# Two weight slabs per modulation product instead of one, in a two-layer diffusion transformer kernel

## The chip, the cores and the metric

The kernel runs on one core of one Trainium2 chip. The metric is the device time of one launch in microseconds (us). Three runs of the kernel before gave 2456.32, 2459.8 and 2463.0 us; the median is 2459.8 us. In the tables TensorE is PE (its weight loads PEld), VectorE is DVE, ScalarE is ACT, GpSimd is POOL, and SyncE is SP, which issues the transfers (DMAs).

## What is computed

Two layers run over 512 latent tokens and 256 context tokens, with a model width of 1024. Each layer first makes six modulation vectors for the latent tokens and six for the context tokens (shift, scale and gate of two sub-layers) out of one conditioning vector each:

```python
silu_c = jax.nn.silu(c)
silu_cc = jax.nn.silu(c_ctx)
...
mx = (silu_c @ w_ada[i] + b_ada[i])[:, None, :]
mc = silu_cc @ w_ada[i] + b_ada[i]
sx1, ax1, gx1, sx2, ax2, gx2 = jnp.split(mx, 6, axis=-1)
...
hx = modulate(rmsnorm(x, norm1_g[i]), sx1, ax1)
...
x = x + gx1 * y_x
x = x + gx2 * sqrelu_mlp(modulate(rmsnorm(x, norm2_g[i]), sx2, ax2), w_mlp1[i], w_mlp2[i])
```

`w_ada[i]` is 1024 x 6144 float32. It is 24 slabs of 1024 x 256, of 1 MB each, for a layer, so 48 in all. Between them stand the large products: the input projection, a differential attention, a depthwise convolution, two gate projections, two output projections, and an MLP of width 4096.

## The kernel before

**Weights.** Every large weight is read in slabs of 1 MB. `load_slab` (line 84) issues the transfer into a buffer with the tag "raw" (named `r_...`), and then splits it in two halves: ACT copies a half to a rounded part (`h_...`), and DVE or POOL subtracts that from the raw half (`l_...`). Products take three passes (`mm3`, lines 104 to 106): L104 and L105 need only `h_...`, L106 needs `l_...`. The tags of `h_...` and `l_...` have two buffers each. A modulation slab is not split: `raw_slab` (line 79) loads it, into the same tag "raw", as `ada...`, and the products read it from there.

**The raw buffers.** From the gate projections of layer 0 to the end of its MLP the tag "raw" has two buffers (`state["nraw"]` is 2, set at line 857), shared by the weight slabs and the modulation slabs. A buffer that held a weight slab is free when its split is done (DVE or POOL reads it last). A buffer that held a modulation slab is free when its eight products on PE are done.

**One modulation slab** (`ada_slab`, line 209): load it; eight products of 32 columns by 256 into a PSUM bank, `adaps`; ACT copies that to SBUF, `adasb`; two transposes on PE into the other half of the bank; DVE sums four strips with two reductions and adds the bias.

**Where the slabs stand.** Slabs 0 to 7 of layer 0 come first of all. Slabs 8 to 15 stand in the middle of the eight gate slabs (`wg`, line 941), 16 to 19 at the four slabs of the attention's output projection (`wao`), and 20 to 23 at the convolution's two (`wco`). The 24 slabs of layer 1 stand in the MLP of layer 0: two after the first two slabs of `w_mlp1`, and then one after each slab of `w_mlp1` (product `f`) and `w_mlp2` (product `r`), until none is left. In layer 1 there are none.

**What sets the order.** The framework's scheduler, which simulates a timeline (line 1287), orders the instructions of each engine and hands out the buffers; each engine and the queue of SP then run in the order written. An MLP slab has 96 matrix instructions: 2 blocks of columns by 8 rows by 3 passes for 512 tokens, and as many for 256.

Of the kernel before, what the change touches and what calls it, by code (L numbers as in the profile page):

```python
# [14 lines left out]
P = 128  # L15
# [36 lines left out]
def trunk_kernel(  # L52
# [153 lines left out]
        L["A2"] = lpool.tile([P, 2, KT], F32, tag="A2", name=f"A2{i}")  # L206
        return L

    def ada_slab(i, L, s):

        mi = state["mi"]
        r = raw_slab(rows(w_ada[i], 256 * s, 256), f"ada{i}_{s}")
        ps = mi(f"adaps{i}_{s}")
        for k in range(KT):
            j = k % 4
            nc.tensor.matmul(ps[32 * j : 32 * j + 32, :256], cvec[:, k, :], r[:, k, :],
                             start=k < 4, stop=k >= 4, tile_position=(0, 32 * j))
        if state["nt"] == 3:
            sb = state["tp"].tile([P, 512], F32, tag="t2k", bufs=3, name=f"adasb{i}_{s}")[:, :256]
        else:  # L220
            sb = spool.tile([P, 512], F32, tag="dg", name=f"adasb{i}_{s}", bufs=1)[:, :256]
        nc.scalar.activation(out=sb, in_=ps[:, :256], func=AF.Copy)
        pc = ps[:, 256:512]
        for m in range(2):
            nc.tensor.transpose(pc[:, m * P : m * P + P], sb[:, m * P : m * P + P], ident)
        ad = L["ad"][:, :, 2 * s : 2 * s + 2]
        for q in range(2):
            nc.vector.tensor_reduce(
                out=ad[:, q], in_=pc.rearrange("p (m j r) -> p m j r", m=2, j=4)[:, :, :, q],
                axis=AX.X, op=ALU.add)  # L230
        nc.vector.tensor_tensor(
            out=ad, in0=ad,
            in1=L["cols"][:, R_BADA + 2 * s : R_BADA + 2 * s + 2].unsqueeze(1)
            .to_broadcast([P, 2, 2]),
            op=ALU.add)

    def ada_gain(L, which, ks=slice(0, KT)):
        par, r0, nm = ((1, R_N1, "A1"), (4, R_N2, "A2"))[which]
# [121 lines left out]
                (w_qk[0][:, k, :], w_qk[1][:, k, :]), k == 0, k == KT - 1)  # L360

    for q in range(4):
        ada_slab(0, L, 4 + q)
        ada_slab(0, L, q)
        ada_gain(L, 0, slice(2 * q, 2 * q + 2))
        for k in (2 * q, 2 * q + 1):
            for s, g in ((0, LAT), (1, CTXS)):
                nc.vector.tensor_scalar(XN[:, k, g], XN[:, k, g], L["A1"][:, s, k : k + 1],
                                        L["ad"][:, s, k : k + 1], ALU.mult, ALU.add)
                split(hh[:, k, g], hl[:, k, g], XN[:, k, g])  # L370
        if q:
            qk_part(2 * q - 2)
            qk_part(2 * q - 1)
# [13 lines left out]
    for i in range(DEPTH):  # L387
# [532 lines left out]
        for half, lst in ((1, ga), (0, gc)):  # L920
            for s in range(4):
                if (half, s) not in wg:
                    gate_slab(half, s)
                if half == 0 and s == 3:
                    for hg in branch[:4]:
                        branch_load(*hg)
                w = wg.pop((half, s))
                for m in range(2):
                    mb = 2 * s + m
                    t = g3(f"g{i}_{half}_{mb}")  # L930
                    lst[mb] = t
                    for g in groups:
                        W = g.stop - g.start
                        ps = ps_for(g, f"gt{i}_{half}_{mb}_{g.start}")
                        fm_block(ps[:, :W], w, m * P, lambda k: (hh[:, k], hl[:, k]), g)
                        bcol = R_BG + half * KT + mb
                        nc.scalar.activation(out=t[:, g], in_=ps[:, :W], func=AF.Sigmoid,
                                             bias=cols[:, bcol : bcol + 1])
                    some_taps(per_gate)
                    if m == 0 and not state.get("ada_done"):  # L940
                        ada_slab(i, L, 8 + 4 * half + s)


        cgr = [(0, SEQ, 0)] + ([] if last else [(SEQ + PAD, CTX, SEQ)])
# [55 lines left out]
            split(ah[:, h : h + r.shape[1], g], al[:, h : h + r.shape[1], g], r)  # L1000
        for s in range(4):
            w = load_slab(rows(w_attn_out[i], 256 * s, 256), f"wao{i}_{s}")
            if not state.get("ada_done"):
                ada_slab(i, L, 16 + s)
            for g in groups:
                W = g.stop - g.start
                for m in range(2):
                    mb = 2 * s + m
                    ps = ps_for(g, f"ya{i}_{mb}_{g.start}")
                    fm_block(ps[:, :W], w, m * P, lambda k: (ah[:, k], al[:, k]), g)  # L1010
                    nc.vector.tensor_tensor(out=ga[mb][:, g], in0=ga[mb][:, g], in1=ps[:, :W],
                                            op=ALU.mult)
# [15 lines left out]
        for s in range(2):  # L1028
            w = load_slab(w_conv_out[i][:, 512 * s : 512 * s + 512]
                          .rearrange("(k p) n -> p k n", p=P), f"wco{i}_{s}", shape=(CT, 512))  # L1030
            if not state.get("ada_done"):
                ada_slab(i, L, 20 + 2 * s)
                ada_slab(i, L, 21 + 2 * s)
# [98 lines left out]
        for cch in range(4):  # L1132
# [15 lines left out]
            for s0 in ((0, 2), (2, 3), (3, 4)) if cch == 0 else ((n, n + 1) for n in range(4)):  # L1148
                for s in range(*s0):
                    if (cch, s) not in w1:  # L1150
                        mlp1_slab(cch, s)
                ws = {s: w1.pop((cch, s)) for s in range(*s0)}
                for g in halves if cch == 0 and s0[0] == 0 else groups:
                    for s in range(*s0):
                        for m in range(2):
                            hidden(ws[s], 2 * s + m, m, g)
                if not last and ada_todo:
                    for _ in range(*s0):
                        ada_slab(i + 1, Ln, ada_todo.pop(0))
            fin = cch == 3  # L1160
            if fin and not last:
                ada_gain(Ln, 0)
# [16 lines left out]
                            (w[0][:, k, :], w[1][:, k, :]), k == 0, k == KT - 1)  # L1179

            def after(s):
                if not last and ada_todo:
                    ada_slab(i + 1, Ln, ada_todo.pop(0))
                if fin and not last:
                    nc.sync.dma_start(xs_d[i + 1][:, 2 * s : 2 * s + 2, :],
                                      X[:, 2 * s : 2 * s + 2, :])
                if fin and last:
                    for t in range(4):
                        ps = state["mi"](f"oT{s}_{t}")
                        for m in range(2):  # L1190
# [17 lines left out]
                 lambda: first.update(v=v_slab(i + 1, 0, nc.gpsimd))) if fin and not last else ())  # L1208
        if not last:
            while ada_todo:  # L1210
                ada_slab(i + 1, Ln, ada_todo.pop(0))
            state["ada_done"] = True
            ada_gain(Ln, 1)
            L = Ln
# [77 lines left out]
```

## Time and profile before

One execution was profiled. "Span" is the time from its first instruction to its last.

| | us |
|---|---|
| median of three runs | 2459.8 |
| profiled execution, device time | 2461.13 |
| its span | 2459.3 |
| mean granted clock of TensorE over the span | 0.978 of full |
| PE idle, longest waits by line: gate product for `l_wg` from POOL, 2 times | 26.9 |
| PE idle before the first `yc` product of layer 1, once | 6.4 |

In the timeline a row gives the start, the duration, the engine, the source line, the operation, what it writes and reads, its shape and how many were merged; in brackets stands how long the engine sat idle before it, and who released it. One product of 32 columns by 256 shows as two records. A row of the windows view gives, for a stretch of the span, the busy time of each engine with its number of instructions, the granted clock of TensorE (PEclk, 1.00 is full) and the share of the DMA engines.

### The profile page before, as it was taken

The numbers are of one execution on the slowest core, as the hardware profiler recorded it, in microseconds if no ns is written. First come the engines' busy times: TensorE is split into PE (matmuls) and PEld (weight loads), VectorE is DVE, ScalarE is ACT, GpSimd is POOL, SyncE is SP. The second block draws the span as 40 slices with busy tenths as digits, with TensorE's granted clock in tenths as the row PEclk, the third lists the DMA queues.
The fourth block names the chain that finished last, engine by engine and source line by source line (L and its number), as shares of the span: only waits on it lengthen the run. The fifth ranks groups of instructions, "written<-read, shape, count | busy, mean of one in ns | idle before, by whom it ended". The sixth has DMA issues, their size and how long they took to land. (4 is left out here: it accounts for less than half of the span.)

```text
span 2459.3 us, 36996 instructions
## 1 busy us (share of the span) xinstructions
PE 2332.2 (95%) x15034; PEld 2066.7 (84%) x15034; DVE 1341.4 (55%) x2307; ACT 946.8 (38%) x1839; POOL 745.3 (30%) x1038
## 2 busy tenths in 40 slices
PE   7999999979999999999999998999896989999999
PEld 6889988868878988888888997989875869888887
DVE  6767776589657452222222356676747966533333
ACT  5556565512324242231312345555641323522331
POOL 2856665150000042120211255666614000200100
PEclk9999999989999999999999999999998999999999
DMA  9101111124444233333333221111113323323322
GB/s 299 55 27 46 42 43 43 43 95 156 132 141 157 84 104 103 121 119 113 112 120 103 73 66 54 42 42 42 59 56 101 118 91 104 103 86 103 96 92 69
DMA packets 222186, 224.79 MB, mean 91 GB/s; under 512 B 5872, under 2 KB 212160, under 8 KB 221888
## 3 DMA queue, kind: packets, MB, share of 16 engines
q1 hardware_dynamic: 222016, 222.43, 28.5%
q8 instruction: 118, 1.93, 0.3%
q14 instruction: 52, 0.43, 0.1%
HBM read 208.73 MB, written 13.67 MB: 90 GB/s over the span
## 5 line engine op out<-in xcount | busy, mean ns | idle before, releaser
L104 PE MATMUL f<-h2h,h_w 128*128 128x512 f32 (+1 forms) x832 | 284.8, 345 | 1.3 <-ACT h2h L76 1.0
L104 PE MATMUL r<-fh,h_w 128*128 128x512 f32 (+1 forms) x832 | 285.5, 344 | 0.5 <-DVE X L1072 0.5
L105 PE MATMUL f<-h2l,h_w 128*128 128x512 f32 (+1 forms) x832 | 284.9, 343 | 0.9 <-POOL h2l L77 0.8
L105 PE MATMUL r<-fl,h_w 128*128 128x512 f32 (+1 forms) x832 | 283.2, 341 | 0.0
L106 PE MATMUL r<-fh,l_w 128*128 128x512 f32 (+1 forms) x832 | 283.2, 341 | 0.0
L106 PE MATMUL f<-h2h,l_w 128*128 128x512 f32 (+1 forms) x832 | 283.1, 342 | 0.0
L76 ACT ACTIVATE h_w<-r_w 128x1024 fp32r<-128x1024 f32 x128 | 128.7, 1052 | 314.0 <-PE r L105 131.1
L1141 POOL TENSOR_TENSOR fr<-fr 128x512 f32<-128x512 f32 (+1 forms) x104 | 93.1, 897 | 509.5 <-ACT fh L1140 509.5
L887 DVE SCALAR_TENSOR_TENSOR cacc<-z,cols,cacc 128x783 f32<-128x783 f32 (+1 forms) x240 | 203.4, 902 | 0.5
L104 PE MATMUL qk<-h_wqk,h1h 128*128 128x256 f32 x640 | 185.5, 292 | 8.7 <-ACT rw L479 4.2
L105 PE MATMUL qk<-l_wqk,h1h 128*128 128x256 f32 x640 | 182.6, 287 | 0.0
L104 PEld LDWEIGHTS f<-h2h,h_w 128*128 128x128 f32 x832 | 158.0, 191 | 25.1 <-ACT fh L1140 2.5
L1072 DVE SCALAR_TENSOR_TENSOR X<-r,ad,X 128x512 f32<-128x512 f32 (+1 forms) x104 | 64.9, 627 | 208.6 <-PE r L106 208.4
L106 PE MATMUL qk<-h_wqk,h1l 128*128 128x256 f32 x640 | 178.6, 287 | 0.0
L104 PEld LDWEIGHTS r<-fh,h_w 128*128 128x128 f32 x832 | 157.6, 190 | 23.9 <-issue 3.7
L105 PEld LDWEIGHTS f<-h2l,h_w 128*128 128x128 f32 x832 | 159.0, 191 | 20.0 <-POOL h2l L77 2.1
L658 ACT ACTIVATE e<-S,st,rqk 128x768 f32<-128x768 f32 (+1 forms) x160 | 144.9, 908 | 76.5 <-POOL st L655 73.6
L106 PEld LDWEIGHTS f<-h2h,l_w 128*128 128x128 f32 x832 | 158.8, 191 | 17.6
L106 PEld LDWEIGHTS r<-fh,l_w 128*128 128x128 f32 x832 | 157.7, 190 | 17.7
L105 PEld LDWEIGHTS r<-fl,h_w 128*128 128x128 f32 x832 | 157.9, 190 | 17.0
L77 DVE TENSOR_TENSOR l_w<-r_w,h_w 128x1024 fp32r<-128x1024 f32 x106 | 126.2, 1223 | 82.2 <-ACT h_w L76 80.5
L653 DVE TENSOR_REDUCE st<-S 128x1 f32<-128x768 f32 (+1 forms) x160 | 134.0, 846 | 60.3 <-PE S L651 59.1
(248 smaller groups left out, 6254.6 us busy)
## 6 DMA issues: line engine op xcount, KB each, us to landing
r_w<-in_w_mlp_dram SPq DMA_DIRECT2D x64, 1024.0 KB, 5.5
ada<-in_w_ada_dram SPq DMA_DIRECT2D x48, 1024.0 KB, 5.3
r_wqk<-in_w_in_dram SPq DMA_DIRECT2D x32, 512.0 KB, 5.4
r_wg<-in_w_in_dram SPq DMA_DIRECT2D x16, 1024.0 KB, 5.5
r_wv<-in_w_in_dram SPq DMA_DIRECT2D x8, 1024.0 KB, 5.5
r_wao<-in_w_attn_out_dram SPq DMA_DIRECT2D x8, 1024.0 KB, 5.1
r_wo<-in_w_out_dram SPq DMA_DIRECT2D x8, 1024.0 KB, 8.2
at_d<-uo SPq DMA_DIRECT2D x40, 128.0 KB, 1.7
```

The source lines that it names most:

```text
L76: nc.scalar.activation(out=hi, in_=src, func=AF.Copy)
L77: (lo_eng or nc.vector).tensor_tensor(out=lo, in0=src, in1=f32(hi), op=ALU.subtract)
L104: nc.tensor.matmul(ps, sh, mh, start=first, stop=False)
L105: nc.tensor.matmul(ps, sh, ml, start=False, stop=False)
L106: nc.tensor.matmul(ps, sl, mh, start=False, stop=last)
L653: nc.vector.tensor_reduce(out=st[:, m : m + 1], in_=S[:, :nkey], axis=AX.X, op=ALU.max, negate=True)
L658: nc.scalar.activation(out=e[:, :nkey], in_=S[:, :nkey], func=AF.Exp, scale=R[:, t, m : m + 1], bias=st[:, m : m + 1], accum_out=st[:, 2 + ...
L887: nc.vector.scalar_tensor_tensor(out=ca[cc][:, :CV], in0=zt[cc][:, t : t + CV], scalar=wcol, in1=ca[cc][:, :CV], op0=ALU.mult, op1=ALU.add)
L1072: nc.vector.scalar_tensor_tensor(out=X[:, mb, g], in0=ps[:, :W], scalar=gate[:, s, mb : mb + 1], in1=X[:, mb, g], op0=ALU.mult, op1=ALU.add)
L1141: nc.gpsimd.tensor_tensor(out=r[:, :W], in0=r[:, :W], in1=r[:, :W], op=ALU.mult)
```

## The change

Two slabs of `w_ada` are loaded and multiplied together. Their products go side by side into one bank (512 columns), one ACT copy of 512 columns follows, four transposes go to a second bank, and the sums are made for both slabs (in one set of two reductions and one addition where the slabs are neighbours, in two sets in the first stage, which pairs slab 4+q with slab q). The number of products, of transposes and of bytes stays. There are half as many copies.

Each call site now calls for two slabs at every second place: in the gate stage at the odd slabs, in the attention's output projection at the odd slabs, and in the MLP after the even slabs.

```diff
-    def ada_slab(i, L, s):
+    def ada_pair(i, L, ss):
...
-        r = raw_slab(rows(w_ada[i], 256 * s, 256), f"ada{i}_{s}")
-        ps = mi(f"adaps{i}_{s}")
-        for k in range(KT):
-            j = k % 4
-            nc.tensor.matmul(ps[32 * j : 32 * j + 32, :256], cvec[:, k, :], r[:, k, :],
-                             start=k < 4, stop=k >= 4, tile_position=(0, 32 * j))
+        rs_ = [raw_slab(rows(w_ada[i], 256 * s, 256), f"ada{i}_{s}") for s in ss]
+        nm = f"{i}_{ss[0]}"
+        ps = mi(f"adaps{nm}")
+        for n, r in enumerate(rs_):
+            for k in range(KT):
+                j = k % 4
+                nc.tensor.matmul(ps[32 * j : 32 * j + 32, 256 * n : 256 * n + 256], cvec[:, k, :],
+                                 r[:, k, :], start=k < 4, stop=k >= 4,
+                                 tile_position=(0, 32 * j))
...
-        nc.scalar.activation(out=sb, in_=ps[:, :256], func=AF.Copy)
-        pc = ps[:, 256:512]
-        for m in range(2):
+        nc.scalar.activation(out=sb, in_=ps, func=AF.Copy)
+        pc = mi(f"adaT{nm}")
+        for m in range(4):
             nc.tensor.transpose(pc[:, m * P : m * P + P], sb[:, m * P : m * P + P], ident)
...
+        runs = [(0, 4, ss[0])] if ss[1] == ss[0] + 1 else [(0, 2, ss[0]), (2, 4, ss[1])]
...
     for q in range(4):
-        ada_slab(0, L, 4 + q)
-        ada_slab(0, L, q)
+        ada_pair(0, L, (4 + q, q))
...
-                    if m == 0 and not state.get("ada_done"):
-                        ada_slab(i, L, 8 + 4 * half + s)
+                    if m == 0 and s % 2 and not state.get("ada_done"):
+                        ada_pair(i, L, (7 + 4 * half + s, 8 + 4 * half + s))
...
-            if not state.get("ada_done"):
-                ada_slab(i, L, 16 + s)
+            if s % 2 and not state.get("ada_done"):
+                ada_pair(i, L, (15 + s, 16 + s))
...
                 if not last and ada_todo:
-                    for _ in range(*s0):
-                        ada_slab(i + 1, Ln, ada_todo.pop(0))
+                    if s0[0] % 2 == 0:
+                        ada_pair(i + 1, Ln, (ada_todo.pop(0), ada_todo.pop(0)))
...
             def after(s):
-                if not last and ada_todo:
-                    ada_slab(i + 1, Ln, ada_todo.pop(0))
+                if not last and ada_todo and s % 2 == 0:
+                    ada_pair(i + 1, Ln, (ada_todo.pop(0), ada_todo.pop(0)))
```

**The queue of SP in the MLP.** Before, weight slabs and modulation slabs took turns; here from the last slab of the first `w_mlp1` chunk (`r_w1_0_0_3`) on. The brackets name the engine or the transfer whose semaphore the queue waits for.

```order
L90 DMA r_w1_0_0_3_10090<-in_w_mlp1_dram 128x8x256 [waits DMAHW7_49,DMAHW1_49,DVE_49]
L81 DMA ada1_3_10218<-in_w_ada_dram 128x8x256 [waits DMAHW1_49,DVE_49]
L90 DMA r_w2_0_0_0_10236<-in_w_mlp2_dram 128x8x256 [waits DMAHW0_49,PE_49]
L81 DMA ada1_4_10348<-in_w_ada_dram 128x8x256 [waits DMAHW3_49,DVE_49,Pool_49]
L90 DMA r_w2_0_0_1_10366<-in_w_mlp2_dram 128x8x256 [waits DMAHW2_49,PE_49]
L81 DMA ada1_5_10478<-in_w_ada_dram 128x8x256 [waits DMAHW5_49,DVE_49,Pool_49]
```

The same place with the change:

```order
L90 DMA r_w1_0_0_3_10050<-in_w_mlp1_dram 128x8x256 [waits DMAHW0_49,PE_49]
L90 DMA r_w2_0_0_0_10178<-in_w_mlp2_dram 128x8x256 [waits DMAHW1_49,PE_49]
L81 DMA ada1_4_10290<-in_w_ada_dram 128x8x256 [waits DMAHW2_49,DVE_49]
L81 DMA ada1_5_10292<-in_w_ada_dram 128x8x256 [waits DMAHW3_49,DVE_49,Pool_49]
L90 DMA r_w2_0_0_1_10321<-in_w_mlp2_dram 128x8x256 [waits DMAHW4_49,PE_49]
L90 DMA r_w2_0_0_2_10433<-in_w_mlp2_dram 128x8x256 [waits DMAHW5_49,PE_49]
```

Two weight slabs now follow two modulation slabs. The PE event that `r_w2_0_0_1` waits for is, before, the last product of `ada1_3`, which PE runs ahead of all of `r_w2_0_0_0`'s products; with the change it is the last product of `ada1_4`, which PE runs behind them. `r_w2_0_0_2` waits for the last product of `ada1_5`.

**PE at the same place.** Rows of one form and one output are merged (`x8`); `h_w2_0_0_0` is the weight slab just finished, `h_w2_0_0_1` the next one. Before, and the two transposes 22 instructions later:

```order
L106 MATMUL r0_0_1_512_10322<-fh0_0_7_9546,l_w2_0_0_0_10239 128x256
L216 MATMUL adaps1_4_10350<-ada1_4_10348,cvec_328 32x256 x8
L104 MATMUL r0_0_2_0_10374<-fh0_0_0_9532,h_w2_0_0_1_10368 128x512
L105 MATMUL r0_0_2_0_10374<-fl0_0_0_9533,h_w2_0_0_1_10368 128x512
L106 MATMUL r0_0_2_0_10374<-fh0_0_0_9532,l_w2_0_0_1_10369 128x512
```

With the change:

```order
L106 MATMUL r0_0_1_512_10264<-fh0_0_7_9498,l_w2_0_0_0_10181 128x256
L218 MATMUL adaps1_4_10294<-ada1_4_10290,cvec_328 32x256 x8
L218 MATMUL adaps1_4_10294<-ada1_5_10292,cvec_328 32x256 x8
L228 MATMUL adaT1_4_10313<-cst_75,adasb1_4_10311 128x128 x4
L104 MATMUL r0_0_2_0_10329<-fh0_0_0_9484,h_w2_0_0_1_10323 128x512
L105 MATMUL r0_0_2_0_10329<-fl0_0_0_9485,h_w2_0_0_1_10323 128x512
L104 MATMUL r0_0_3_0_10355<-fh0_0_0_9484,h_w2_0_0_1_10323 128x512
L105 MATMUL r0_0_3_0_10355<-fl0_0_0_9485,h_w2_0_0_1_10323 128x512
L104 MATMUL r0_0_2_512_10381<-fh0_0_0_9484,h_w2_0_0_1_10323 128x256
L105 MATMUL r0_0_2_512_10381<-fl0_0_0_9485,h_w2_0_0_1_10323 128x256
L104 MATMUL r0_0_3_512_10407<-fh0_0_0_9484,h_w2_0_0_1_10323 128x256
L105 MATMUL r0_0_3_512_10407<-fl0_0_0_9485,h_w2_0_0_1_10323 128x256
```

Both slabs' products and all four transposes now stand together between two weight slabs, and the passes that need only `h_...` (L104, L105) of four blocks come ahead of the first L106. The same picture stands at eleven places of layer 0's MLP, for the pairs (2,3) to (22,23).

**PE in the gate stage.** `gt` is the gate product, and `wg0_1_3` the gate slab under way; with the change:

```order
L106 MATMUL gt0_1_6_512_6744<-h1h_0_334,l_wg0_1_3_6712 128x256
L218 MATMUL adaps0_14_6781<-ada0_14_6777,cvec_328 32x256 x8
L218 MATMUL adaps0_14_6781<-ada0_15_6779,cvec_328 32x256 x8
L104 MATMUL gt0_1_7_0_6809<-h1h_0_334,h_wg0_1_3_6711 128x512
L105 MATMUL gt0_1_7_0_6809<-h1l_0_335,h_wg0_1_3_6711 128x512
```

Here the pair stands in the middle of a weight slab: 48 products of `wg0_1_3` (24 for 512 tokens, 24 for 256) are still behind it. The next slab, `r_wg0_0_0`, waits for the last product of `ada0_14`; before, it waited for a split on DVE.

More of the change, by code (lines that the diff above doesn't have):

```diff
@@ L218, in ada_slab @@
         if state["nt"] == 3:
-            sb = state["tp"].tile([P, 512], F32, tag="t2k", bufs=3, name=f"adasb{i}_{s}")[:, :256]
+            sb = state["tp"].tile([P, 512], F32, tag="t2k", bufs=3, name=f"adasb{nm}")
         else:
-            sb = spool.tile([P, 512], F32, tag="dg", name=f"adasb{i}_{s}", bufs=1)[:, :256]
-        nc.scalar.activation(out=sb, in_=ps[:, :256], func=AF.Copy)
-        pc = ps[:, 256:512]
-        for m in range(2):
+            sb = spool.tile([P, 512], F32, tag="dg", name=f"adasb{nm}", bufs=1)
@@ L225, in ada_slab @@
+        nc.scalar.activation(out=sb, in_=ps, func=AF.Copy)
+        pc = mi(f"adaT{nm}")
+        for m in range(4):
             nc.tensor.transpose(pc[:, m * P : m * P + P], sb[:, m * P : m * P + P], ident)
[L226 to L235, printed above, removed]
+        pcv = pc.rearrange("p (m j r) -> p m j r", m=4, j=4)
@@ new lines, in ada_pair @@
+        runs = [(0, 4, ss[0])] if ss[1] == ss[0] + 1 else [(0, 2, ss[0]), (2, 4, ss[1])]
+        for a, b, s in runs:
+            ad = L["ad"][:, :, 2 * s : 2 * s + b - a]
+            for q in range(2):
+                nc.vector.tensor_reduce(out=ad[:, q], in_=pcv[:, a:b, :, q], axis=AX.X, op=ALU.add)
+            nc.vector.tensor_tensor(
+                out=ad, in0=ad,
+                in1=L["cols"][:, R_BADA + 2 * s : R_BADA + 2 * s + b - a].unsqueeze(1)
+                .to_broadcast([P, 2, b - a]),
+                op=ALU.add)
@@ L1031, in trunk_kernel @@
             if not state.get("ada_done"):
-                ada_slab(i, L, 20 + 2 * s)
-                ada_slab(i, L, 21 + 2 * s)
+                ada_pair(i, L, (20 + 2 * s, 21 + 2 * s))
             for m in range(4):
@@ L1210, in trunk_kernel @@
             while ada_todo:
-                ada_slab(i + 1, Ln, ada_todo.pop(0))
+                ada_pair(i + 1, Ln, (ada_todo.pop(0), ada_todo.pop(0)))
             state["ada_done"] = True
```

## The prediction

> **What bounds the kernel now.** I read the page first: its table of busy time, and the slices of the span.
>
> ```profile
> PE 2332.2 (95%) x15034; PEld 2066.7 (84%) x15034; DVE 1341.4 (55%) x2307; ACT 946.8 (38%) x1839; POOL 745.3 (30%) x1038
> ...
> PEclk9999999989999999999999999999998999999999
> DMA  9101111124444233333333221111113323323322
> ```
>
> PE is the bound, and the transfers are far from one. Next I asked the windows view about the two stretches that hold most of the edited code: the gate stage of layer 0 (570 to 690) and layer 0's MLP with the slabs of layer 1 (905 to 1316).
>
> ```profile
> core 0: us, PE busy (x) PEld busy (x) DVE busy (x) ACT busy (x) POOL busy (x), PEclk, DMA share, GB/s
> 570.00:690.00 120.00, 120.00 (x751) 101.81 (x749) 90.10 (x118) 34.64 (x54) 0.00 (x0) 1.00 0.48 152
> ...
> 905.00:1316.00 411.00, 411.00 (x2579) 349.38 (x2578) 107.35 (x195) 97.78 (x158) 71.94 (x58) 1.00 0.37 117
> ```
>
> In both PE is busy in every microsecond, at full clock. So whatever PE must wait for here is added to the time, and what the other engines save is worth nothing. The waits in the MLP stretch say who has slack:
>
> ```profile
> ACT adasb L222 <- PE adaps L216: 120.5, 21, 11.0
> DVE ad L228 <- PE adaps L225: 109.7, 22, 5.8
> ACT h_w L76 <- DMA r_w<-in_w_mlp_dram: 94.5, 19, 5.5
> ```
>
> ACT and DVE wait for the modulation products, not the other way round. The third row is the one that matters: ACT waited 19 times, 94.5 us in all, for a weight slab to land, and PE did not feel it, since it was working on the slab before. The change takes that cover away.
>
> **The chain behind a weight load.** This is one modulation slab of the MLP in the timeline (columns: start, duration, engine, line, operation):
>
> ```profile
> 1273.70 0.37 SPq L90 DMA_DIRECT2D r_w<-in_w_mlp_dram  x1
> ...
> 1290.35 0.28 PE L105 MATMUL r<-fl,h_w 128*128 128x256 f32 x1
> 1290.47 0.28 PE L106 MATMUL r<-fh,l_w 128*128 128x256 f32 x1
> 1290.68 1.07 PE L216 MATMUL adaps<-ada,cvec 128*32 128x256 f32 x16
> 1291.68 0.50 PE L104 MATMUL r<-fh,h_w 128*128 128x512 f32 x1
> 1291.81 0.37 SPq L90 DMA_DIRECT2D r_w<-in_w_mlp_dram  x1
> 1292.02 0.40 PE L105 MATMUL r<-fl,h_w 128*128 128x512 f32 x1
> ...
> 1296.35 0.40 PE L106 MATMUL r<-fh,l_w 128*128 128x512 f32 x1
> 1296.58 0.38 PE L225 MATMUL adaps<-cst,adasb 128*128 128x128 f32 x2
> 1296.72 0.48 PE L104 MATMUL r<-fh,h_w 128*128 128x512 f32 x1
> 1297.04 0.39 PE L105 MATMUL r<-fl,h_w 128*128 128x512 f32 x1
> 1297.27 0.40 PE L106 MATMUL r<-fh,l_w 128*128 128x512 f32 x1
> ...
> 1297.51 2.01 ACT L76 ACTIVATE h_w<-r_w 128x1024 fp32r<-128x1024 f32 x2 [5.24 <-DVE ad L231]
> ...
> 1298.60 1.23 DVE L77 TENSOR_TENSOR l_w<-r_w,h_w 128x1024 fp32r<-128x1024 f32 x1 [1.09 <-ACT h_w L76]
> ```
>
> At 1290.68 PE starts the eight products of a slab; when the last is done, SP issues the next weight load (1291.81); ACT starts the split 5.7 us later, and its first half is done at 1298.60, when DVE takes over. So from the first modulation product to the first `h_w` that PE can use pass 1298.60 - 1290.68 = **7.92 us**. In this kernel PE spends them on the slab it already has. The queue's issues lie 1291.81 - 1273.70 = 18.1 us apart, so the load has a slab's time to spare.
>
> **What the change adds.** By the queue's order above, the odd weight slab after a pair now takes the buffer of the pair's first slab, and waits for that slab's products. PE runs those behind the last product of the weight slab before. So at each of the eleven places (pairs 2-3 to 22-23) the 7.92 us begin when PE has only the pair itself left to do. Nothing else can fill in: the rows behind all need the slab that is still to come. The landing behind it, of the even slab, shares the DMA engines but is issued second and is needed a slab later. What `l_w` needs, DVE's 1.23 us, is covered: eight products that use `h_w` alone stand first, four of 512 columns (0.23 apart, 1297.04 to 1297.27) and four of 256 (0.12 apart, 1290.35 to 1290.47), 1.4 us. The pair itself, and four transposes, show in the first stage:
>
> ```profile
> 14.65 0.60 PE L324 MATMUL xT<-cst,xr 128*128 128x128 f32 x4
> ...
> 44.44 1.93 PE L216 MATMUL adaps<-ada,cvec 128*32 128x256 f32 x32
> ```
>
> PE has 1.93 + 0.60 = 2.5 us of work in the 7.92, and idles some 5.4. Against before: one slab costs PE 1.20 us for the products (1291.68 less 1290.59, when the next row would have started, and 0.11 for a first row that takes 0.34 in place of 0.23) and 0.23 for the transposes (0.14 and 0.09 likewise), 1.43 in all, so 2.86 for two. Now the place costs 7.92 and 0.2 for the two changes of form, 8.12. Net **5.26 us at each of eleven places: 57.9 us**. The transfer sets the bounds:
>
> ```profile
> DMA to landing us min/median/max: 5.0/5.5/5.8
> ```
>
> That is 0.5 less or 0.3 more at a place, -6 to +3 in all.
>
> **The clock after the wait.** The granted clock falls after idle stretches of this kind. Two of them, with the stretch that followed:
>
> ```profile
> 54.85 0.38 PE L104 MATMUL qk<-h_wqk,h1h 128*128 128x256 f32 x1 [3.55 <-ACT h1h L76]
> ...
> 2019.44 0.80 PE L113 MATMUL yc<-ch,h_wco 128*128 128x512 f32 x1 [6.41 <-ACT ch L992]
> ```
>
> ```profile
> 2019.50:2025.30 5.80, 5.80 (x14) 4.60 (x15) 3.63 (x6) 2.18 (x4) 0.00 (x0) 0.50 0.52 174
> ...
> 55.85:59.26 3.41, 3.41 (x18) 3.41 (x17) 1.26 (x3) 0.08 (x1) 0.00 (x0) 0.50 0.21 57
> 59.30:62.70 3.40, 3.40 (x30) 3.32 (x29) 0.42 (x1) 1.51 (x5) 0.23 (x1) 1.00 0.92 247
> ```
>
> After 3.55 us idle, 3.41 us ran at 0.50, with 18 products where 30 fit at full clock: 1.4 us lost. After 6.41 us idle, 5.80 us of work ran at 0.50: 14 products that take 3.2 us at full clock (0.23 each), 2.6 lost. An idle time of 5.4 lies between; I take 2.0 us, **22 us** in all, with 1.4 and 2.6 as bounds (15 and 29). The Trainium skill's page "TensorE: Matmul & The Clock Gate", in the section "What's actually happening", has the half clock come after an idle window of about 3.4 us and end after one busy window of that length; by that rule no wait would cost more than the 1.4, and the sum would be 7 us less. The stretch of 5.80 us at 0.50 speaks against that rule here, so I keep the rows.
>
> **What the change saves.** Where PE is not kept waiting, a pair costs 1.20 + 0.86 (the 1.93 less the 1.07 of one slab) for the products and 0.37 for four transposes (0.14 twice, and 0.09), 2.43 in place of 2.86. That holds for nine pairs: four in the gate stage, two at `wao`, two at `wco`, and the pair 0-1 of layer 1, **-3.9 us** (at the least 0). In the first stage PE waits for others, and I count nothing. The saved ACT and DVE time lies beside PE, by the first rows of waits, and is worth nothing.
>
> **The other places with the new wait.** In the gate stage the pair stands in mid-slab. Behind its first products PE has 0.86, the transposes' 0.37 and half a weight slab, 24 x 0.23 + 24 x 0.12 = 8.4, together 9.6 us. The chain asks for 7.92, and for `l_wg` 1.23 more before the third product (0.45 later): 8.7. It fits with 0.9 us to spare, if DVE is free; DVE runs convolution taps there (90.1 of 120 us busy), so I allow up to 2 us at each of four places. At `wao` the pair 16-17 stands with 44 products behind it, nearly all of 256 columns: 5.3 + 0.86 + 0.37 = 6.5 against 8.7, so some 2 us late. At `wco` and `wo` a whole slab covers the load. I take **+2 us** (0 to 10).
>
> **The sum**, against the profiled execution: 2461.1 + 57.9 + 22 - 3.9 + 2 = 2539.1 us. The median of the three runs stands 1.3 us lower, so **2538 us**, 3.2% slower. All lower bounds together (52, 15, -3.9, 0) give 2523, all upper ones (61, 29, 0, 10) 2560.
>
> **Rivals.**
> - *Faster.* If the odd slab's load were released one weight slab earlier, 18.1 us before it is needed, the 7.92 would stay hidden, as they are now, and only the savings would be left: 0.43 at twenty pairs outside the first stage, 8.6 us, so 2451 us, 0.35% faster. The point that decides is whether PE has more than 7.92 us of other products queued behind the pair's first slab; in the gate stage it has 9.6. Against it stand the queue's waits in the MLP, and that the scheduler itself put the transposes ahead of the next slab's products. A rule for the change belongs here: the Trainium skill's page "VectorE: DVE Perf Modes", section "The TRN2 errata", has one large tile pay an instruction's fixed latency once where small tiles pay it each time. That can only shorten ACT's and DVE's share, for which PE does not wait by the rows of waits. Chance 0.03.
> - *No change.* Only some savings and a few waits that cancel them; it needs the same early release at all but one of the eleven places: about 2459. Chance 0.02.
> - *Milder.* PE waits at about half the places, because the products of a pair's first slab run ahead inside a weight slab; 2461 + 40 - 6, near 2495. At the pair 2-3 seven of the eight do run ahead, but the eighth stands behind the slab, and at the other ten places all eight do. Chance 0.06.
> - *Heavier.* The gate stage waits as well: if DVE comes late to `l_wg`, four more places cost up to 7.3 each, 29 us, near 2567. Chance 0.07.
>
> That the change does not do what it says can be ruled out: the instruction order shows the pairs.
>
> **Chances and range.** The forecast, eleven waits at their bounds, has 0.82. The range, 2515 to 2565, holds it and the lower part of the heavier case; it leaves out most of the two milder ones and of the faster one. A measurement of this kernel tells about 0.3% (7.4 us) from no change. Faster by more than that 0.03, within it 0.02, slower by more 0.95.
>
> **What would show it.** In the profile after: PE idle about 5.4 us ahead of an L104 with `h_w`, eleven times between 900 and 1400 us, ended by ACT's `h_w` split; the half clock some 4 us behind each; PE below full busy in that stretch, which is some 80 us longer; `r_w` issued in twos within 1 us, 0.1 us behind the pair's products; gate stage and layer 1 as before. The prediction is wrong if the `r_w` loads are issued a slab earlier than the pair's products, if PE idles in the gate stage by more than 10 us, or if the clock stays at 1.00 after waits of 5 us.

## The result and the profile after

The changed kernel takes 2533.55 us (median of 4 runs, 2532.97 to 2534.91), the kernel before 2458.12 us in the runs that go with it: a ratio of **1.0307**, with a 95% interval of 1.0292 to 1.0322. The profiled execution of the changed kernel has a span of 2532.2 us, 72.9 more than before.

The page of the changed kernel, with the rows that were shown of before:

```profile
PE 2348.7 (93%) x15034; PEld 2083.7 (82%) x15034; DVE 1329.9 (53%) x2247; ACT 944.6 (37%) x1815; POOL 750.9 (30%) x1038
...
PEclk9999999989999999999999999999997999999999
DMA  8101111133544132424233122111113233232231
```

There are 60 instructions fewer on DVE and 24 fewer on ACT, as the change says, and PE has as many as before, yet it is busy 16.5 us longer: the same products, some at a lower clock. The windows view, for the stretch that stands in place of the prediction's 570 to 690 and for the MLP of layer 0 (the columns are those of the windows rows above):

```profile
580.00:700.00 120.00, 119.61 (x746) 102.48 (x746) 91.46 (x114) 35.75 (x53) 0.00 (x0) 1.00 0.43 138
...
905.00:1400.00 495.00, 439.69 (x2607) 374.42 (x2607) 100.49 (x164) 97.34 (x145) 72.94 (x60) 0.93 0.31 98
```

From 580 on PE works nearly without a pause; the gate stage as a whole begins at 494.8, and its long wait lies before 580 (see the gate stage's wait below). In the MLP stretch it stands still for 495.0 - 439.7 = 55.3 us, and the mean clock is 0.93; before, it was busy in every microsecond there, at 1.00. The waits of PE in that stretch (total, times, longest), and the largest of SP's queue:

```profile
PE r L104 <- ACT h_w L76: 24.7, 6, 4.2
PE f L104 <- ACT h_w L76: 22.5, 5, 4.6
PE adaT L228 <- ACT adasb L225: 8.1, 11, 0.8
...
SPq L90 <- PE adaps L218: 311.4, 22, 30.0
```

Eleven times PE waits 4.1 to 4.6 us for a new weight slab's split, and as often 0.7 us for the copy that the transposes read. The weight loads (L90) wait for the modulation products, which is the wait that the prediction names. One place in the timeline:

```profile
1228.73 1.93 PE L218 MATMUL adaps<-ada,cvec 128*32 128x256 f32 x32
...
1229.86 1.23 SPq L90 DMA_DIRECT2D r_w<-in_w_mlp_dram  x2
...
1230.73 0.60 ACT L225 ACTIVATE adasb<-adaps 128x512 f32<-128x512 f32 x1 [1.06 <-PE adaps L218]
...
1231.38 0.66 PE L228 MATMUL adaT<-cst,adasb 128*128 128x128 f32 x4 [0.72 <-ACT adasb L225]
...
1235.44 2.00 ACT L76 ACTIVATE h_w<-r_w 128x1024 fp32r<-128x1024 f32 x2 [4.11 <-DMA r_w<-in_w_mlp_dram]
...
1236.55 0.80 PE L104 MATMUL f<-h2h,h_w 128*128 128x512 f32 x1 [4.51 <-ACT h_w L76]
```

The first load is issued when the first slab's eight products are done; 5.6 us later it has landed and ACT starts the split; its first half is done at 1236.5, and PE goes on. From the pair's first product to there pass 1236.55 - 1228.73 = 7.82 us. The first product then takes 0.80 us in place of some 0.5, and the two stretches behind it show why:

```profile
1236.60:1242.30 5.70, 5.70 (x16) 4.64 (x17) 4.65 (x4) 2.84 (x3) 0.00 (x0) 0.50 0.58 182
1242.40:1248.10 5.70, 5.70 (x27) 4.69 (x26) 0.00 (x0) 0.12 (x1) 0.00 (x0) 1.00 0.72 235
```

5.7 us run at half clock, with 16 products where 27 follow in the same time. Cut at the first product of each stage, the two traces stand so (us; the gate stage is 496.0 to 675.2 before and 494.8 to 676.9 after):

| stage | before | after | difference |
|---|---|---|---|
| up to the first gate product of layer 0 | 496.0 | 494.8 | -1.2 |
| gate stage | 179.2 | 182.1 | +2.9 |
| attention's output projection (`wao`) | 82.3 | 78.3 | -4.0 |
| `wco`, `wo` | 107.6 | 107.5 | -0.1 |
| layer 0's MLP | 607.3 | 685.6 | **+78.3** |
| layer 1 | 986.9 | 983.9 | -3.0 |

The MLP carries all of the loss. Its 78.3 us are 55.3 of idle PE (57.1 against 1.8), 26.3 of half clock (half of the time that PE was busy at 0.50: 28.0 against 1.7), less 3.3 that the pairs save in PE's own work (the busy time with its half-clock share taken off, 603.8 and 600.4).

### The profile page after: what moved, and what is told of

It is laid out like the page before. It is cut to its first block, busy times and chain, and to the rows that moved or that the text cites. A ratio compares the mean times of both kernels' runs of the same rounds, so it can differ in the third digit from the quotient of the medians.

```text
span 2532.2 us, 36844 instructions
## 1 busy us (share of the span) xinstructions
PE 2348.7 (93%) x15034; PEld 2083.7 (82%) x15034; DVE 1329.9 (53%) x2247; ACT 944.6 (37%) x1815; POOL 750.9 (30%) x1038
## 3 DMA queue, kind: packets, MB, share of 16 engines
q1 hardware_dynamic: 222016, 222.43, 27.4%
## 5 line engine op out<-in xcount | busy, mean ns | idle before, releaser
L104 PE MATMUL r<-fh,h_w 128*128 128x512 f32 (+1 forms) x832 | 290.2, 350 | 25.2 <-ACT h_w L76 24.7
L104 PE MATMUL f<-h2h,h_w 128*128 128x512 f32 (+1 forms) x832 | 289.6, 351 | 23.8 <-ACT h_w L76 22.5
L105 PE MATMUL f<-h2l,h_w 128*128 128x512 f32 (+1 forms) x832 | 289.8, 349 | 1.1 <-POOL h2l L77 1.0
L105 PE MATMUL r<-fl,h_w 128*128 128x512 f32 (+1 forms) x832 | 288.8, 347 | 0.0
L106 PE MATMUL f<-h2h,l_w 128*128 128x512 f32 (+1 forms) x832 | 283.4, 345 | 0.0
L106 PE MATMUL r<-fh,l_w 128*128 128x512 f32 (+1 forms) x832 | 283.2, 343 | 0.0
L104 PEld LDWEIGHTS r<-fh,h_w 128*128 128x128 f32 x832 | 162.2, 195 | 46.2 <-ACT h_w L76 26.2
L104 PEld LDWEIGHTS f<-h2h,h_w 128*128 128x128 f32 x832 | 161.9, 196 | 45.8 <-ACT h_w L76 23.7
L1144 DVE TENSOR_TENSOR fl<-fr,fh 128x512 fp32r<-128x512 f32 (+1 forms) x104 | 62.5, 604 | 259.1 <-POOL fr L1143 259.0
L104 PE MATMUL qk<-h_wqk,h1h 128*128 128x256 f32 x640 | 182.9, 288 | 6.1 <-ACT h1h L76 2.9
L105 PEld LDWEIGHTS f<-h2l,h_w 128*128 128x128 f32 x832 | 162.8, 196 | 22.5 <-POOL h2l L77 2.5
L105 PE MATMUL qk<-l_wqk,h1h 128*128 128x256 f32 x640 | 180.2, 284 | 0.0
L106 PE MATMUL qk<-h_wqk,h1l 128*128 128x256 f32 x640 | 177.0, 284 | 0.6 <-DVE h1l L77 0.6
L105 PEld LDWEIGHTS r<-fl,h_w 128*128 128x128 f32 x832 | 162.2, 195 | 18.5
L106 PEld LDWEIGHTS f<-h2h,l_w 128*128 128x128 f32 x832 | 159.6, 193 | 18.2
L106 PEld LDWEIGHTS r<-fh,l_w 128*128 128x128 f32 x832 | 158.9, 192 | 18.1
```

The lines of the kernel that those rows point to most:

```text
L104: nc.tensor.matmul(ps, sh, mh, start=first, stop=False)
L105: nc.tensor.matmul(ps, sh, ml, start=False, stop=False)
L106: nc.tensor.matmul(ps, sl, mh, start=False, stop=last)
L1144: nc.vector.tensor_tensor(out=fl[mb][:, g], in0=r[:, :W], in1=f32(fh[mb][:, g]), op=ALU.subtract)
```

## Experiments

The theory is the prediction's: the odd weight slab behind a pair takes the buffer of the pair's first slab, so its load waits for products that PE runs when it has nothing else left, and the clock falls behind that wait. The rivals are that the computation by pairs costs the time (the 512-column bank, the one copy, four transposes in a row), that the place of the pair does, or that the loss is outside the MLP. Ten kernels were run; their table stands behind the first seven.

**Two single slabs in place of a pair.** In the MLP only, at the pairs' places:

```diff
                     if s0[0] % 2 == 0:
-                        ada_pair(i + 1, Ln, (ada_todo.pop(0), ada_todo.pop(0)))
+                        for _ in range(2):
+                            ada_slab(i + 1, Ln, ada_todo.pop(0))
...
-                    ada_pair(i + 1, Ln, (ada_todo.pop(0), ada_todo.pop(0)))
+                    for _ in range(2):
+                        ada_slab(i + 1, Ln, ada_todo.pop(0))
```

> In layer 0's MLP two single modulation slabs stand at each place of a pair, each with its own eight products, its own copy of 256 columns, its own two transposes and its own bank; the loads stand in the queue as with the pairs. Theory (the loads' order: the odd weight slab's load waits for the first modulation slab's products, which PE runs behind the whole weight slab before): the eleven waits stay, 4 to 5 us each, and the time stays at 2525 to 2545 us. Rival (the computation by pairs: the 512-column bank, the one copy, four transposes in a row, the second bank): the MLP goes back to the time of before, 2450 to 2462 us.

Measured: 2524.37 us, ratio 1.0272 (1.0258 to 1.0286). PE's waits in that MLP:

```profile
PE r L104 <- ACT h_w L76: 26.1, 6, 4.9
PE f L104 <- ACT h_w L76: 22.7, 5, 4.6
PE adaps L257 <- ACT adasb L254: 5.9, 11, 0.5
```

The same eleven waits, and an MLP of 685.8 us, without any bank that two slabs share. The computation by pairs isn't the cause. The 9 us by which this kernel is faster than the changed one lie in layer 1 (974.6 us against 983.9; see the table below).

**Single slabs in the MLP, pairs elsewhere.** In the first half of the MLP (in the second half likewise):

```diff
-                    if s0[0] % 2 == 0:
-                        ada_pair(i + 1, Ln, (ada_todo.pop(0), ada_todo.pop(0)))
+                    for _ in range(*s0):
+                        ada_slab(i + 1, Ln, ada_todo.pop(0))
```

> Single slabs in layer 0's MLP, one behind each weight slab, as before the change; pairs everywhere else. Theory: all of the loss is in the MLP, 78 us by the two traces (607.3 us before, 685.6 after), so 2452 to 2460 us, with a gate stage some 3 us longer and an attention output projection some 4 us shorter than before the change. Rival (part of the loss is elsewhere, or layer 1 is hurt by what is left behind): above 2465 us.

Measured: 2454.01 us, 0.9987 (0.9978 to 0.9996). The MLP is back at 607.3 us; gate stage 182.0, `wao` 78.9.

**The pair in the middle of its weight slab.** In the MLP, behind the columns for 512 tokens of the even slab, ahead of those for 256 (in the second half likewise):

```diff
+                            if (not last and ada_todo and s0[1] - s0[0] == 1 and s % 2 == 0 and m
+                                    and g is groups[0]):
+                                ada_pair(i + 1, Ln, (ada_todo.pop(0), ada_todo.pop(0)))
```

> Pairs as in the change, but in the MLP each stands in the middle of its even weight slab, so that 48 products (24 of 512 columns, 24 of 256, 8.4 us) of that slab are still behind the pair's first products. Theory: the chain of 7.8 us from a pair's first product to the odd slab's first split half is covered by 8.4 + 0.9 + 0.4 = 9.7 us of products, no wait over 1 us is left in the MLP, the clock stays at 1.00, and each pair saves 0.43 us: 2533.5 - 78.3 - 4.7 = 2450 us, 2446 to 2457. Rival (pairs cost by themselves, wherever they stand): 2500 us or more.

Measured: 2443.37 us, 0.9948 (0.9934 to 0.9963). The MLP by the windows view:

```profile
860.30:1465.40 605.10, 601.94 (x4024) 533.49 (x4024) 188.52 (x330) 172.36 (x305) 148.64 (x134) 1.00 0.33 105
```

3.2 us idle in all, and the clock at 1.00: the same pairs cost nothing where PE has half a weight slab behind them. They save 2.2 us and not the 4.7 that were expected here.

**The pair's loads behind the load of the odd slab.** The call stands behind the load of the odd weight slab and ahead of its products (in the second half of the MLP likewise):

```diff
+                if not last and ada_todo and s0[1] - s0[0] == 1 and s0[0] % 2:
+                    ada_pair(i + 1, Ln, (ada_todo.pop(0), ada_todo.pop(0)))
                 for g in halves if cch == 0 and s0[0] == 0 else groups:
```

> Pairs as in the change, but in the MLP the pair's two loads stand behind the load of the odd weight slab, not ahead of it, and its products ahead of the odd slab's products. Theory: the odd slab's load then waits only for a split that is long done, and the next even slab's load waits for the pair's products with a whole weight slab (17 us) to cover it: no waits, 2450 us, 2446 to 2457. Rival (the wait moves to the pair itself, whose loads now wait for the odd slab's split and land late, so that PE stands before the pair's products): 2480 us or more, with waits ahead of the modulation products.

Measured: 2444.36 us, 0.9944 (0.993 to 0.9958):

```profile
862.00:1464.50 602.50, 600.66 (x4024) 534.08 (x4024) 201.06 (x330) 172.69 (x305) 144.34 (x134) 1.00 0.33 105
```

The MLP takes 602.5 us, with 1.8 idle. Here the pair's products do stand behind a whole weight slab, as in the change; only the order in the queue, and with it who takes which buffer, differs.

**A buffer of its own for the first slab of a pair.** Call sites as in the change:

```diff
+        def own(s):
+            t = [state["tp"].tile([P, 512], F32, tag="t2k", bufs=4, name=f"ada{i}_{s}_{k}")
+                 .rearrange("p (k n) -> p k n", k=2) for k in range(4)]
+            for k in range(4):
+                nc.sync.dma_start(t[k], rows(w_ada[i], 256 * s, 256)[:, 2 * k : 2 * k + 2])
+            return lambda k: t[k // 2][:, k % 2]
...
+        rs_ = [own(s) if i and n == 0 else shared(s) for n, s in enumerate(ss)]
```

> The change with one thing different: in the MLP the first slab of a pair goes, in four transfers of 256 KB, into four 2-KB buffers of another tag that the MLP leaves unused, so that of the two raw buffers a pair takes only one. The call sites, the 512-column product, the copy and the four transposes stay. Theory (the shared buffer is the wait): the odd weight slab's load then waits for a split that is long done, the eleven waits go, and the time falls to 2446 to 2460 us. Rival (where PE runs the pair, behind a whole weight slab, costs the time, whatever the buffers do): 2520 us or more.

Measured: 2441.55 us, 0.9943 (0.9924 to 0.9961):

```profile
861.40:1464.30 602.90, 601.07 (x4025) 534.31 (x4025) 189.01 (x330) 171.49 (x305) 144.77 (x134) 1.00 0.33 104
```

With the queue's order and the place of the pair as in the change, and one buffer more, the waits and the half clock are gone: 602.9 us. Together with the two singles this settles the cause. It is the shared buffer, not the pair.

**PE kept busy in the wait.** The transposes of layer 1's pairs are done ten times over:

```diff
-        for m in range(4):
+        for m in [0, 1, 2, 3] * (10 if i and ss[0] else 1):
             nc.tensor.transpose(pc[:, m * P : m * P + P], sb[:, m * P : m * P + P], ident)
```

> The change with the four transposes of each pair of layer 1 done ten times over, into the same bank with the same values: 36 more of some 0.09 us, 3.3 us, in the 4.3 us in which PE waits for the odd weight slab. Theory (the half clock follows from PE's idle time): the chain behind the load keeps its length, so the eleven places end as late as before, but the clock stays up: of the 26 us that the half clock costs in this MLP most is saved, 2505 to 2515 us, and the granted clock there is 1.00 or close. Rival (the half clock comes from the restart on a fresh slab, or the transposes delay the next slab): 2530 us or more.

Measured: 2501.35 us, 1.0186 (1.017 to 1.0203). PE's waits, and the MLP as a whole:

```profile
PE adaT L228 <- ACT adasb L225: 8.0, 11, 0.8
PE f L104 <- ACT h_w L76: 3.1, 5, 0.8
PE r L104 <- ACT h_w L76: 3.0, 5, 1.3
```

```profile
863.50:1527.00 663.50, 647.39 (x4421) 577.78 (x4421) 200.24 (x330) 174.07 (x305) 143.97 (x134) 1.00 0.30 96
```

396 more transposes, and the MLP is 22.1 us *shorter* than in the changed kernel (685.6): PE gets the odd slab about as late (by 26.3 - 22.1 = 4.2 us over eleven places, 0.4 later at each), but the clock stays at 1.00, and the half clock's cost falls from 28.0 to 1.7 us, what it was before the change. The half clock is the price of the idle time itself.

**Pairs in the MLP alone.** The other call sites as before the change, for instance:

```diff
-            if s % 2 and not state.get("ada_done"):
-                ada_pair(i, L, (15 + s, 16 + s))
+            if not state.get("ada_done"):
+                ada_slab(i, L, 16 + s)
```

> Pairs in layer 0's MLP alone, single slabs in the first stage, the gate stage and at the two output projections, as before the change. Theory (by the stages of the two traces the pairs outside the MLP gave -1.2, +2.9, -4.0 and -0.1 us): 2533.5 + 2.4 = 2536 us, 2530 to 2542, with the 3.5-us wait at the attention's output projection back and the gate stage's wait for POOL near 13 us, not 18. Rival (the pairs outside the MLP do more for or against than their stages show): outside 2526 to 2546.

Measured: 2535.7 us, 1.0323 (1.0305 to 1.034). Two of PE's waits between the gate stage and `wco`:

```profile
PE gt L106 <- POOL l_wg L77: 12.9, 1, 12.9
...
PE ya L104 <- ACT h1h L76: 3.4, 1, 3.4
```

Both are what they were before the change (12.9 and 3.5), and the MLP is 685.6 us. So outside the MLP the pairs made POOL's wait longer and took away the one at `wao`.

The kernels so far, in us, from their traces (the MLP from the first `f` product to the first `kc`, which opens layer 1; the gate stage from its first product to the first `ya`):

| kernel | median | MLP | idle in it | lost to half clock | layer 1's gate stage |
|---|---|---|---|---|---|
| before | 2458.1 | 607.3 | 1.8 | 1.7 | 103.9 |
| the change | 2533.6 | 685.6 | 57.1 | 28.0 | 104.2 |
| two singles | 2524.4 | 685.8 | 56.5 | 27.4 | 87.0 |
| single in the MLP | 2454.0 | 607.3 | 1.8 | 1.7 | 103.9 |
| mid-slab | 2443.4 | 605.1 | 3.2 | 1.7 | 87.0 |
| behind the next load | 2444.4 | 602.5 | 1.8 | 1.7 | 87.0 |
| own buffer | 2441.6 | 602.9 | 1.8 | 1.7 | 87.0 |
| filled wait | 2501.4 | 663.5 | 16.1 | 1.7 | 87.0 |
| MLP alone | 2535.7 | 685.6 | 57.9 | 27.2 | 104.2 |

In five runs the time lies below the expected range: by 0.6 us in the two singles, 2.6 in mid-slab, 1.6 behind the next load, 4.5 with the own buffer, 3.7 with the filled wait. The last column shows most of the reason: in these kernels a wait of 14 to 15 us in layer 1's gate stage is missing, while the attention ahead of it takes 4 to 12 us more than before; layer 1 as a whole is 3 to 11 us shorter than in the changed kernel. None of that is in the code that was edited, and what moves it stays open. So the total times of these kernels hold a part that their edits are not shown to cause; the cause of the loss is read from the MLP column.

**The gate stage's wait.** These rows are from the timeline of layer 0's gate stage: POOL's two subtractions, the last of DVE's work in a row (taps of the convolution, each one multiply-and-add), PE's next product, and what DVE does next, before the change and then after.

```profile
520.63 25.47 POOL L77 TENSOR_TENSOR l_wg<-r_wg,h_wg 128x1024 fp32r<-128x1024 f32 x2 [9.93 <-ACT h_wg L76]
...
540.54 1.02 DVE L887 SCALAR_TENSOR_TENSOR cacc<-z,cols,cacc 128x783 f32<-128x783 f32 x1
...
543.82 0.80 PE L106 MATMUL gt<-h1h,l_wg 128*128 128x512 f32 x1 [12.89 <-POOL l_wg L77]
...
553.88 0.24 DVE L228 TENSOR_REDUCE ad<-adaps 128x2 f32<-128x8 f32 x2 [12.31 <-PE adaps L225]
```

```profile
519.57 30.80 POOL L77 TENSOR_TENSOR l_wg<-r_wg,h_wg 128x1024 fp32r<-128x1024 f32 x2 [9.95 <-ACT h_wg L76]
...
541.99 3.85 DVE L890 SCALAR_TENSOR_TENSOR cacc<-z,cols,cacc 128x783 f32<-128x783 f32 x4
...
548.10 0.80 PE L106 MATMUL gt<-h1h,l_wg 128*128 128x512 f32 x1 [18.23 <-POOL l_wg L77]
...
565.98 1.22 DVE L77 TENSOR_TENSOR l_wg<-r_wg,h_wg 128x1024 fp32r<-128x1024 f32 x1 [20.14 <-ACT h_wg L76]
```

Both times PE goes on 2.3 us after DVE's last convolution tap (541.56 and 545.84), and 2.4 us is what the shorter of POOL's two subtractions takes (the longer takes 23.1 before and 28.5 after the change). DVE ran without a pause up to there. So it looks as if POOL gets nowhere until DVE rests. Before, DVE rested when it came to the sums of the first modulation slab of this stage, whose products PE had not reached; with the change these stand one weight slab later, and DVE goes on with taps until 545.84. To test it, the subtraction goes to DVE, in the mid-slab kernel:

```diff
-            gate_slab(1, 0, nc.gpsimd)
+            gate_slab(1, 0)
...
-            gate_slab(1, 1, nc.gpsimd)
+            gate_slab(1, 1)
```

> Pairs in mid-slab in the MLP, and the low halves of the first two gate slabs of each layer made by VectorE in place of GpSimd. It tests the gate stage's wait, 12.9 us before the change and 18.2 after. Theory (one GpSimd subtraction takes 25 to 28 us there, in place of 2.4, because VectorE runs its two-input convolution taps without a pause): the wait of 18.2 us in layer 0 and the half clock behind it (4 us) go, 2443 - 22 = 2421 us, 2414 to 2430. Rival (VectorE gets to the subtraction only behind the taps that are queued, and the wait stays): 2438 us or more.

Measured: 2419.76 us, 0.9852 (0.9834 to 0.9869). Layer 0's gate stage:

```profile
519.13 2.34 DVE L77 TENSOR_TENSOR l_wg<-r_wg,h_wg 128x1024 fp32r<-128x1024 f32 x2
...
495.90:652.00 156.10, 156.10 (x997) 135.09 (x996) 137.07 (x159) 41.30 (x63) 0.83 (x1) 1.00 0.43 139
```

The two subtractions take DVE 2.34 us, PE has no idle time left, and the stage falls from 182 to 156 us. Then the same edit was made in the kernel before, and in the kernel with the buffer of its own, to see what of this is owed to pairs.

> The kernel before, single slabs everywhere, with only the low halves of the first two gate slabs on VectorE. It tells how much of the gain of the mid-slab pairs with that edit (2420 us) is owed to pairs. From the stages of the traces: layer 0's gate stage 179 to 156 us, layer 1's 104 to 87 us. Theory (where layer 1's gate wait goes, its attention gets some 8 us longer, as it did in every run so far without that wait): 2455 - 23 - 17 + 8 = 2423 us, 2418 to 2430, so pairs are worth some 4 us, in the attention's output projection and the MLP. Rival (pairs are worth nothing or the attention does not lengthen): 2413 to 2418 us.

Measured: 2419.93 us, 0.9856 (0.9835 to 0.9877). The expectation was met in the total, not in its reason: layer 1's gate stage is 87.0 us, but its attention did not get longer (389.1 against 388.9 before); what comes ahead of `wao` took 3.7 us more than in the mid-slab kernel with the same edit, 2.3 of them in layer 0's gate stage (158.4 us). The wait at `wao` is 1.3 us here, without any pair, so pairs are not the only thing that shortens it.

> The change with the first slab of a pair in buffers of its own in the MLP, and the low halves of the first two gate slabs on VectorE. Theory (the two edits act at different places and add up): an MLP of 603 us and a gate stage of 156, 2441.5 - 24 = 2418 us, 2413 to 2424. Rival (they share a resource and do not add up): 2430 us or more.

Measured: 2417.01 us, 0.9843 (0.9825 to 0.9862), the lowest of all, with an MLP of 601.4 us. The intervals of the three overlap: single slabs as before, with the gate edit, are about as fast as pairs with it. All three beat both kernels, by the gate edit.

## Why the prediction was right

**The forecast and its terms.** 2538 us was forecast, 2533.6 measured. For the MLP the terms were 57.9 of waits, 22 of half clock and -0.4 for the pair 0-1, 79.5 in all; the trace has 78.3. The division between the two is less good: waits less savings came to 55.3 - 3.3 = 52.0 us, and the half clock to 26.3. Both lie inside their bounds (52 to 61, 15 to 29), the first only just, and their errors of -5.9 and +4.3 nearly cancel. That the total came so close is in part luck.

**The chain.** 7.92 us were taken from a single slab's timeline, and the place shown has 7.82. It is one of the longest: the eleven places have 7.4 to 7.9, 7.6 on average. The idle time was put at 5.4 us a place; it is 4.3 ahead of the slab and 0.7 ahead of the transposes, 5.0. Its cause, count (eleven) and place are as forecast, and the own buffer shows the cause.

**The clock.** 2.0 us a place was chosen between 1.4 and 2.6; it is 26.3 / 11 = 2.4. In the clock's record eight of the eleven stretches at 0.50 last 6.83 us and three 3.41. Which of the two is told by when PE goes on: 0.14, 0.30 and 0.36 us into a stretch where it lasts 3.41, and 0.73 to 2.2 us into it where it lasts 6.83. The 22 places of the two singles and of the MLP alone part the same way, 3.41 up to 0.44 us and 6.83 from 0.64 us on. So the clock seems to come back at the end of the first 3.41 us that PE works through nearly from their start. The Trainium skill's page "TensorE: Matmul & The Clock Gate", section "What's actually happening", has the windows run free of what the kernel does, and one busy window bring the full clock back; with that these stretches agree. The prediction took from it that no wait would cost more than 1.4 us; that was a wrong reading, since a restart within a window costs the rest of that window too. Its row of 5.80 us at 0.50 does not speak against the rule either: that half clock lasted from 2015.10 to 2025.34, three times 3.41 us, and PE went on at 2019.44, 0.9 us into the second of the three.

**The places outside the MLP.** Here steps failed, by small amounts. At `wao` the prediction had the weight load come 2 us late; in the trace no load is late, both `r_wao` are issued together (at 667.27) ahead of the pair's loads, and the 3.5-us wait of before (`ya` for `h1h`, so for the attention's output and not for a slab) is down to 0.4, with no half clock behind it: -4.0. In the gate stage the cover behind the pairs held, PE was busy 119.6 of 120 us from 580 on, so the heavier rival did not come. But the stretch that the prediction called the gate stage, from 570 on, leaves out the stage's first 74 us and the 12.9-us wait for POOL in them. What happened there no step foresaw: that wait grew by 5.3 us, and the half clock behind it cost 0.6 more, against 3.1 saved in PE's own work (1.7 forecast), +2.9 in all. Over the whole stage PE idles 21.8 us, against 16.4 before; more than 10 us of idle time there was named as a sign that the prediction is wrong, and by the whole stage it would have shown before the change already. The savings of the pairs at `wco` do not show (-0.1 for two pairs, -0.9 forecast). Layer 1 was forecast to stay as it was; it has -3.0. All in all the stages outside the MLP gave -5.4, where -1.5 was forecast (-3.5 and +2): 3.9 of the 5.1 us by which the forecast's 78.0 exceeds the 72.9 between the spans.

**The rivals.** Faster asked for a load that is released a slab earlier. The kernel with the loads behind the next slab's is that case, and its MLP of 602.5 us shows that the price worked out for it was near: 12 pairs at 0.43 us are 5.2, and the order of loads decides between -4.8 and +78.3 us in this stage. The two rivals between, milder and no change, needed places without the wait; all eleven have it.

## What to carry to other kernels

When loads of two kinds share a small ring of buffers, ask for each load which earlier user it waits for and when the bottleneck engine will have run that user; grouping two small users can put that point behind all the work that covered the load. A saving on engines that nobody waits for is worth nothing against that. Give the small loads a buffer of their own, issue them behind the next large load, or put them where the bottleneck engine has more work queued than the load takes: here each of the three took the whole loss away.

## What was not expected of the hardware

A GpSimd subtraction of 128 x 1024 took 2.3 to 3.4 us or 23.1 to 28.5 us, with nothing in its operands changed, mostly by whether VectorE paused beside it. Thirteen of them in the traces are of the long kind, and each ended 2.20 us after the end of VectorE's unbroken row of work. Layer 1's gate stage shows it from both sides. First the changed kernel, where VectorE does not pause, then the mid-slab kernel, where it does, for 0.65 us:

```profile
1936.23 27.44 POOL L77 TENSOR_TENSOR l_wg<-r_wg,h_wg 128x1024 fp32r<-128x1024 f32 x2 [8.77 <-ACT h_wg L76]
```

```profile
1862.30 5.81 POOL L77 TENSOR_TENSOR l_wg<-r_wg,h_wg 128x1024 fp32r<-128x1024 f32 x2 [8.64 <-ACT h_wg L76]
1863.67 2.17 DVE L446 TENSOR_TENSOR z<-z,sg 128x512 f32<-128x512 f32 x1 [0.65 <-ACT sg L444]
1865.77 4.21 DVE L890 SCALAR_TENSOR_TENSOR cacc<-z,cols,cacc 128x512 f32<-128x512 f32 x3
```

In the second case VectorE pays instead: 2.17 us for an operation that takes 0.68 elsewhere, and 1.4 for a tap of 0.7. The Trainium skill's page "SBUF — State Buffer", section "Who interferes with whom", has a VectorE instruction with two SBUF inputs and a reading GpSimd instruction exclude each other, and the order of issue decide which of them waits. The rows agree, with one addition: in the thirteen cases GpSimd did not get in between two instructions of the row, but waited for its end. One kind of row let it in. Layer 0's first two subtractions took 2.95 and 3.13 us with VectorE busy throughout:

```profile
490.33 6.04 POOL L77 TENSOR_TENSOR l_wg<-r_wg,h_wg 128x1024 fp32r<-128x1024 f32 x2 [0.40 <-ACT h_wg L76]
490.33 0.69 DVE L446 TENSOR_TENSOR z<-z,sg 128x512 f32<-128x512 f32 x1
490.93 0.42 DVE L77 TENSOR_TENSOR wtl<-wT,wth 128x256 fp32r<-128x256 f32 x1
491.26 7.01 DVE L890 SCALAR_TENSOR_TENSOR cacc<-z,cols,cacc 128x783 f32<-128x783 f32 x3
```

Here one VectorE instruction, `wtl`, has an input in PSUM (`wT`), and 2.35 us from its start at 490.93 the first subtraction ends. So it looks as if GpSimd got in beside it; that was not tried by itself. What shifts VectorE's pause from kernel to kernel was not tried either.

The other surprise is the filled wait: 396 useless transposes made the changed kernel 32 us faster. Some 22 us of that are in the MLP, because PE's clock did not fall; most of the rest is in layer 1, where the gate stage's wait is missing as in the table above.
